# A two-block network on one core: how small work is spread between the weight products

## The chip, the cores and the metric

One Trainium2 chip, one core. The time is the device time of one execution, in microseconds (us). Before the change: median 1421.77 us of 3 runs (1421.32 to 1427.34). TensorE is PE, its weight loads PEld, VectorE DVE, ScalarE ACT, GpSimd POOL, SyncE SP.

## The reference

Two transformer blocks run one after the other on 256 tokens of width 1024; each has 2 layers, all in float32.

```
first block, per layer:
  z = rmsnorm(h) @ w_in + b_in          # conv, pool, q, k, v, gates, index
  ya = conv31 -> layer norm -> silu -> matmul, times silu(gate)
  yb = windowed mean - value -> group matmul, times silu(gate)
  yc = attention over the 64 keys of highest index score, times silu(gate)
  h += concat(ya, yb, yc) @ w_out
  h += (p @ ple_w) * sigmoid(h @ ple_gate_w)
  at the end h = rmsnorm(h)
second block, per layer (x: 256 tokens, ctx: 256 tokens):
  mod = silu(c) @ w_ada + b_ada
  u = modulate(rmsnorm(x)) @ w_in
  gated linear attention (forward and backward), short conv, neighbourhood attention
  x += g1 * concat(...) @ w_out
  x += g2 * convffn(modulate(rmsnorm(x)))
  the same for ctx in layer 0; at the end x = rmsnorm(x)
```

## The kernel before

Features lie on the partitions, tokens along the free axis (T = 256). Each float32 product is made of three products of rounded parts (`mm3`, L387 to L390: high by high, high by the rest of the data, rest of the weight by high). Weights arrive in units of 128x1024 float32 (512 KB) that SP loads into a ring of 4 (`rawunit`, L425); ACT copies a unit to its high part (L441) and DVE subtracts to get the rest (`hl`, L449). This subtraction is called the split. A tile of the output is 24 products (8 blocks of the inner size, three each). The third product of a block (L390) needs the split; the first two need ACT's copy alone.

Beside these tiles there is small work: in the first block the convolution (31 taps of two DVE operations each, `conv1`, L951), the pooling, the index scores and the attention; in the second the linear attention (`gla`, L1466) and the neighbourhood attention (`na`, L1666). Each is a generator that yields a number, its portion's cost. After every weight tile the main loop calls `tick` (L467), which runs portions until a budget is used:

```
    def tick(s, budget=1500.0, feed=True):
        ...
        while budget > 0 and s.tasks:
            for g in list(s.tasks):
                ...
                    c = next(g)
                ...
                if c is not None:
                    budget -= c
```

What is left is drained by `until` and by `flush` (L496), with no weight tile between its portions. So the budget, the yields and the place of a `tick` set how small work and weight tiles follow each other, and a tile framework then orders each engine's instructions; a "pinned" instruction keeps its place.

In the first block's `layer1` (L738) the last eight tiles of the input projection are gates (loop over j, a tick after each). Then w_out is applied in two halves of its inner size: g=0 takes the four blocks that are ready early, g=1, after `flush`, the convolution and the last attention heads. Each half adds its own result to h.

The sums of squares for the norms (`sumsq_add`, L528) are squares by ACT and additions `sqa` (L537), at the second block's residual by POOL; POOL takes the power -0.5 (L519). The merge of the linear attention (about L1650) adds both directions, squares, reduces over 64 columns (`gss`), takes the power on POOL (`grr`), multiplies (`slO`, L405) and transposes the tile on PE (L1660).

## Time and profile before

| | before |
|---|---|
| median of 3 runs | 1421.77 us |
| profiled execution | 1419.99 us |
| its span | 1418.2 us |
| granted clock, mean | 0.984 |
| PE busy | 1363.1 us (96%), 10658 products |
| DVE busy | 1126.9 us (79%) |
| ACT busy | 675.8 us (48%) |
| POOL busy | 69.1 us (5%) |

The profile comes from one execution. Busy time is the time with an instruction in work; a wait is idle time on an engine with the instruction that ended it. PE is the engine with the least idle time, so the list of its waits is the list of what can be had without taking products away. The granted clock is 1.00 where PE runs at 2.4 GHz and 0.50 where it runs at 1.2 GHz.

### The profile page before, as it was taken

Reading aid. Unit: us, or ns where it says so; the run is one execution under the profiler, and the core shown is the slowest. Engines: PE = TensorE matmul, PEld = TensorE weight load, DVE = VectorE, ACT = ScalarE, POOL = GpSimd, SP = SyncE. Lnnn points to the kernel's source line nnn. Section 1 sums busy time; section 2 is a strip of 40 time slices with the busy share of each in tenths; the row PEclk is TensorE's granted clock in tenths of the full one; section 3 lists DMA queues with packets and bytes.
Section 4 is the critical chain, followed back from the end, with each engine's and each line's share of the span. In section 5 each row is a group of like instructions: output and inputs, shape, how many; then the busy total and the mean of one; then the engine's idle time right before and its main releaser. Section 6 shows DMA issues by size and latency. Waiting matters only on the chain.

```text
span 1418.2 us, 26810 instructions
## 1 busy us (share of the span) xinstructions
PE 1363.1 (96%) x10658; PEld 1167.0 (82%) x10658; DVE 1126.9 (79%) x2382; ACT 675.8 (48%) x1258; POOL 69.1 (5%) x98
## 2 busy tenths in 40 slices
PE   8999899997999998999999999999999999999997
PEld 7878799787988776778888888888788877999997
DVE  6998669997889776888788977888767556798794
ACT  4446465464763343546444313343255446565562
POOL 0000000000100001011000000001210000100001
PEclk9999899998999999999999999999999999999999
DMA  7974256333643433432444564557732232376562
GB/s 263 333 248 132 90 164 219 108 118 120 208 148 121 137 100 97 143 102 80 143 137 153 159 189 149 165 183 254 231 117 91 92 116 89 119 217 195 183 194 73
DMA packets 63909, 219.02 MB, mean 154 GB/s; under 512 B 7270, under 2 KB 12328, under 8 KB 63528
## 3 DMA queue, kind: packets, MB, share of 16 engines
q1 hardware_dynamic: 58368, 209.22, 45.9%
q10 hardware_dynamic: 5416, 8.09, 1.7%
q8 instruction: 84, 1.38, 0.4%
q14 instruction: 41, 0.34, 0.1%
HBM read 216.23 MB, written 1.05 MB: 153 GB/s over the span
## 4 chain that ended last, share of the span: by engine, by line
PE 71%; DVE 14%; issue 6%; DMA 4%; ACT 3%; POOL 2%; ACTq 0%; POOLq 0%; DVEq 0%
PE mm L388 20%; PE mm L389 19%; PE mm L390 19%; PE ax L385 8%; DVE hl L449 3%; DMA wada<-in_wadaT_dram 2%; PE mm L385 1%; DVE wada L683 1%; DMA raw<-in_units_dram 1%; PE ada L385 1%; DVE gU L396 1%; PE ax L1744 1%; ACT hl L441 1%; DVE x L396 1%; POOL sqa L537 1%
## 5 line engine op out<-in xcount | busy, mean ns | idle before, releaser
L388 PE MATMUL mm<-xx,hl 128*128 128x256 f32 (+1 forms) x1720 | 555.5, 325 | 5.5 <-ACT xx L414 2.0
L390 PE MATMUL mm<-xx,hl 128*128 128x256 f32 (+1 forms) x1720 | 545.5, 318 | 1.5 <-DVE hl L449 1.4
L389 PE MATMUL mm<-xx,hl 128*128 128x256 f32 (+1 forms) x1720 | 546.3, 318 | 0.0
L441 ACT ACTIVATE hl<-raw 128x1024 fp32r<-128x1024 f32 x286 | 301.4, 1055 | 189.1 <-PE mm L390 152.0
L449 DVE TENSOR_TENSOR hl<-raw,hl 128x1024 fp32r<-128x1024 f32 x286 | 349.4, 1223 | 46.8 <-ACT hl L441 45.2
L388 PEld LDWEIGHTS mm<-xx,hl 128*128 128x128 f32 x1720 | 324.7, 189 | 50.2 <-issue 16.7
L390 PEld LDWEIGHTS mm<-xx,hl 128*128 128x128 f32 x1720 | 325.4, 190 | 30.3 <-DVE hl L449 3.1
L389 PEld LDWEIGHTS mm<-xx,hl 128*128 128x128 f32 x1720 | 325.7, 190 | 27.7 <-issue 4.7
L396 DVE SCALAR_TENSOR_TENSOR y<-mm,sp,y 128x255 f32<-128x255 f32 (+1 forms) x184 | 109.1, 595 | 31.4 <-ACT y L409 30.1
L389 PE MATMUL mm<-hid,hl 128*128 128x256 f32 (+1 forms) x374 | 124.8, 334 | 0.0
L388 PE MATMUL mm<-hid,hl 128*128 128x256 f32 (+1 forms) x374 | 124.0, 332 | 0.0
L390 PE MATMUL mm<-hid,hl 128*128 128x256 f32 (+1 forms) x374 | 123.9, 331 | 0.0
L683 DVE CUSTOM_DVE_ANT_0 wada<-wada,crow,sp 128x1024 f32<-128x1024 f32 x80 | 103.9, 1305 | 10.7 <-DMA wada<-in_wadaT_dram 10.3
L409 ACT ACTIVATE y<-mm,sp 128x256 f32<-128x256 f32 (+1 forms) x92 | 60.6, 659 | 98.4 <-PE mm L390 98.3
L388 PEld LDWEIGHTS mm<-hid,hl 128*128 128x128 f32 x374 | 71.8, 192 | 7.7
L389 PEld LDWEIGHTS mm<-hid,hl 128*128 128x128 f32 x374 | 71.8, 192 | 6.7
L390 PEld LDWEIGHTS mm<-hid,hl 128*128 128x128 f32 x374 | 71.5, 191 | 6.9
L396 DVE SCALAR_TENSOR_TENSOR x<-mm,mod,x 128x256 f32<-128x256 f32 x96 | 43.7, 479 | 31.4 <-PE mm L390 31.4
L389 PE MATMUL mm<-hl,xx 128*128 128x416 f32 (+3 forms) x192 | 66.0, 346 | 2.5 <-DVE hl L449 2.5
L537 POOL TENSOR_TENSOR sqa<-sqa,sq 128x256 f32<-128x256 f32 x36 | 35.2, 986 | 673.9 <-ACT sq L409 673.0
L388 PE MATMUL mm<-hl,xx 128*128 128x416 f32 (+3 forms) x192 | 65.9, 349 | 0.1
L390 PE MATMUL mm<-hl,xx 128*128 128x416 f32 (+3 forms) x192 | 65.6, 344 | 0.0
(281 smaller groups left out, 1659.9 us busy)
## 6 DMA issues: line engine op xcount, KB each, us to landing
raw<-in_units_dram SPq DMA_DIRECT2D x296, 512.0 KB, 4.0
wada<-in_wadaT_dram SPq DMA_DIRECT2D x80, 512.0 KB, 3.6
wada<-in_wada_dram SPq DMA_DIRECT2D x16, 512.0 KB, 5.8
nab<-in_nab_dram ACTq DMA_DIRECT2D x12, 192.0 KB, 3.4
crow<-in_crow_dram SPq DMA_DIRECT2D x2, 1024.0 KB, 6.7
x<-in_xT_dram SPq DMA_DIRECT2D x4, 256.0 KB, 5.2
x<-in_ctxT_dram ACTq DMA_DIRECT2D x1, 1024.0 KB, 10.7
c<-in_c_dram ACTq DMA_DIRECT2D x1, 928.0 KB, 5.5
```

What stands on the lines that cost most here:

```text
L385: return s.nc.tensor.matmul(out, lhsT, rhs, start=start, stop=stop, **kw)
L388: s.nc.tensor.matmul(out, l[0], r[0], start=start, stop=False)
L389: s.nc.tensor.matmul(out, l[0], r[1], start=False, stop=False)
L390: s.nc.tensor.matmul(out, l[1], r[0], start=False, stop=stop)
L396: s.nc.vector.scalar_tensor_tensor(out, a, sc, b, op0, op1)
L409: s.nc.scalar.activation(out, in_, func, bias=bias, scale=scale)
L441: a = nc.scalar.activation(hl[:, 0], raw, AF.Copy)
L449: b = nc.vector.tensor_sub(hl[:, 1], raw, hl[:, 0].bitcast(F32))
L537: (eng or s.nc.vector).tensor_tensor(st["acc"], st["acc"], sq, ALU.add)
L683: s.pin(nc.vector.tensor_tensor_reduce(out=w, in0=w, in1=c[:, j], scale=1.0, scalar=bias[:, m : m + 1], op0=ALU.mult, op1=ALU.add, accum_o ...
L1744: nc.tensor.transpose(pt[:, kt * 128 : kt * 128 + 128], L[j][:, kt * 128 : kt * 128 + 128], s.ident)
```

## The change

It has nine parts.

1. Gates of the first block: a tick has a budget of 2800 instead of 1500; the convolution yields after every second tap (1300) and no longer after each (900).
2. First block's w_out: `part` sums both halves in four PSUM banks (three named mm, one ada) that stay open from g=0 to g=1; h gets one addition of 128x512 per pair of output tiles, four in a layer and not sixteen of 128x256. Ticks stand in the first half alone.
3. The norm at the head of a layer works on pairs of blocks, 128x512.
4. The first loads: pinned; the first unit in two pieces; the second and fourth load of x through ACT's queue.
5. The context's sum of squares moves from the gates of layer 1 to the end of layer 0.
6. The last two additions of `sqa` at a residual's sum are made by DVE.
7. The merge of the linear attention yields 800, 700, 400 and 500 where it yielded 1500 and 700.
8. Neighbourhood attention yields 400 between the copies of the probabilities and the products with v, and 500 after them instead of 900.
9. At the end the scale is multiplied in by ACT during the last down projection, so the final step is four multiplications of 128x512. PAIR_PACE, the share of modulation work fed in beside the FFN's upper tiles, goes from 2.2 to 2.7.

```diff
-PAIR_PACE = 2.2
+PAIR_PACE = 2.7
-CONVY = 900
+CONVY = 1300
+GATE_TICK = 2800
-GZ = 1500
+GZ = 800
...
-    def rawunit(s):
+    def rawunit(s, pieces=1):
         u = s.u
         s.u += 1
         raw = s.wp.tile([128, 1024], F32, name=s.nm("raw"), tag="raw", bufs=NRAW)
-        s.nc.sync.dma_start(raw, s.dram[u])
+        n = 1024 // pieces
+        for o in range(0, 1024, n):
+            d = s.nc.sync.dma_start(raw[:, o : o + n], s.dram[u, :, o : o + n])
+            if pieces > 1:
+                s.pin(d)
         return raw
...
+    def part(s, out, hl, ks, off, g):
+        for q, k in enumerate(ks):
+            s_, e_ = not g and not off and q == 0, bool(g) and bool(off) and q == len(ks) - 1
+            r = [s.mv(e, k, 0, T) for e in range(2)]
+            kw = dict(skip_group_check=True)
+            s.mm(out, hl[:, 0, o : o + 128], r[0], s_, False, **kw)
+            s.mm(out, hl[:, 0, o : o + 128], r[1], False, False, **kw)
+            s.mm(out, hl[:, 1, o : o + 128], r[0], False, e_, **kw)
...
-        s.raw0 = []
-        for k in range(0, KT, 2):
-            nc.sync.dma_start(s.h[:, k : k + 2], xT[:, k : k + 2])
-            if k in RAW0:
-                s.raw0.append(s.rawunit())
+
         s.sp1 = s.small1(0)
+        load = lambda q, k: s.pin(q.dma_start(s.h[:, k : k + 2], xT[:, k : k + 2]))
+        load(nc.sync, 0)
+        s.raw0 = [s.rawunit(2)]
+        load(nc.scalar, 2)
+        load(nc.sync, 4)
+        load(nc.scalar, 6)
+        s.raw0.append(s.rawunit())
...
-            for k in range(KT):
-                n = s.t([128, T], "nf", 2, pool=s.sm)
-                s.tt(n, gh[:, k], rs, ALU.mult)
-                s.split(s.xx[:, 1, 0, k], s.xx[:, 1, 1, k], n)
+            for k in range(0, KT, 2):
+                n = s.t([128, 2, T], "nh", 2)
+                s.tt(n, gh[:, k : k + 2], rs.unsqueeze(1).to_broadcast([128, 2, T]), ALU.mult)
+                s.split(s.xx[:, 1, 0, k : k + 2], s.xx[:, 1, 1, k : k + 2], n)
...
         if i == DEPTH - 1:
-            sc = {}
-            for k in range(KT):
-                s.sumsq_add(sc, s.x2[:, k, :T], 2, k == 0, k == KT - 1)
-            rc = s.rstd_cols(sc["ps"][:, 0:2], 2, 1.0 / D, "rc")
...
-            s.tick()
+            s.tick(GATE_TICK)
...
+        wo = [s.bank("mm" if b < 3 else "ada") for b in range(4)]
         for g in range(2):
             if g:
                 s.turns = False
                 s.flush()
-            for m in range(KT):
-                if m % 2 == 0:
-                    hl = s.unit()
-                ps = s.mtile(0, T, hl, WO_ORDER[4 * g : 4 * g + 4], m % 2 * 4)
-                s.tt(h[:, m], h[:, m], ps[:, :T], ALU.add)
+            for m in range(0, KT, 2):
+                hl, ps = s.unit(), wo[m // 2]
+                for d in range(2):
+                    s.part(ps[:, d * T : d * T + T], hl, WO_ORDER[4 * g : 4 * g + 4], d * 4, g)
+                    if not g:
+                        s.tick()
                 if g:
-                    s.split(s.xx[:, 1, 0, m], s.xx[:, 1, 1, m], h[:, m])
-                s.tick()
+                    hm = h[:, m : m + 2]
+                    s.tt(hm, hm, ps.rearrange("p (k t) -> p k t", k=2), ALU.add)
+                    s.split(s.xx[:, 1, 0, m : m + 2], s.xx[:, 1, 1, m : m + 2], hm)
...
+            if i == DEPTH - 2:
+
+                s.sumsq_add(sc, s.x2[:, m, :T], 2, m == 0, m == KT - 1)
+                if m == KT - 1:
+                    s.rc = s.rstd_cols(sc["ps"][:, 0:2], 2, 1.0 / D, "rc")
...
-            yield CONVY
+            if k % 2 == 0:
+                yield CONVY
...
-            for k in range(KT):
-                y = s.x2[:, k, T:]
-                s.stt(y, y, s.sp2[0]["fin"][:, k : k + 1], R[:, :T], ALU.mult, ALU.mult)
-                if k % 2:
-                    q = nc.sync if k % 4 == 1 else nc.scalar
+            for k in range(0, KT, 2):
+                y = s.x2[:, k : k + 2, 0:T]
+                s.tt(y, y, R[:, :T].unsqueeze(1).to_broadcast([128, 2, T]), ALU.mult)
+                q = nc.sync if k % 4 else nc.scalar
...
-                s.sumsq_add(st[j], s.x2[:, m, c], 2, m == 0, m == KT - 1, eng=s.nc.gpsimd if SQP[1] else None)
+                s.sumsq_add(st[j], s.x2[:, m, c], 2, m == 0, m == KT - 1,
+                            eng=s.nc.gpsimd if SQP[1] and m < KT - 2 else None)
...
+                if half and not both:
+
+                    s.a(s.x2[:, m, 0:T], s.x2[:, m, T:], AF.Copy, scale=P["fin"][:, m : m + 1])
...
             yield 700
             rr = s.rstd_cols(ss, 6, 1.0 / 64, "gr")
+            yield 400
             s.tt(o3, o3, rr.unsqueeze(2).to_broadcast([128, 6, 64]), ALU.mult)
+            yield 500
...
                 s.a(PT[j][:, :kw], pt[:, :kw], AF.Copy)
+            yield 400
 
             for kt in range(nkt):
                 for j in range(2):
...
-            yield 900
+            yield 500
```

Three places show how the order of instructions moves. The first is DVE in the gates of layer 0: the rows that end with the split of the fifth gate (`hl_1196` before, `hl_1231` after). `acc` are the taps, `aL` the attention's scores, `py` the pooling, `sil` the gates. Before:

```order
153 L449 TENSOR_TENSOR hl_1123<-raw_1121,hl_1123 128x1024
154 L396 SCALAR_TENSOR_TENSOR sil_942<-th_974,zh_973 128x256
155 L1077 ISA aL_987,amx_986<-ax_984,imk_696 128x128
156 L1077 ISA amx_986 128x1
157 L1077 ISA aL_987,amx_986<-ax_985,imk_696 128x128
158 L1077 ISA amx_986 128x1
159 L396 SCALAR_TENSOR_TENSOR acc_390<-u_206,sp_80,acc_390 128x256 x2
160 L1091 RECIPROCAL asm_1051<-asm_1051 128x2
161 L449 TENSOR_TENSOR hl_1196<-raw_1194,hl_1196 128x1024
```

After:

```order
178 L1104 ISA aL_1153,amx_1152<-ax_1151,imk_689 128x128
179 L1104 ISA amx_1152 128x1
180 L406 TENSOR_TENSOR py_1139<-py_1139,sil_943 128x256
181 L397 SCALAR_TENSOR_TENSOR acc_375<-u_191,sp_72,acc_375 128x256 x3
182 L416 TENSOR_TENSOR xx<-py_1139,xx 128x256
183 L397 SCALAR_TENSOR_TENSOR acc_375<-u_191,sp_72,acc_375 128x256 x3
184 L406 TENSOR_TENSOR yc_1221<-ax_1080,sil_943 128x256
185 L397 SCALAR_TENSOR_TENSOR sil_943<-th_1196,zh_1195 128x256
186 L397 SCALAR_TENSOR_TENSOR acc_375<-u_191,sp_72,acc_375 128x256 x2
187 L454 TENSOR_TENSOR hl_1231<-raw_1229,hl_1231 128x1024
```

Ahead of this split DVE has 62 taps after the change and 30 before, the remaining heads' first scores, and the pooling's products; in layer 1 likewise 32 more.

The second place is PE at w_out in layer 0. `csq`, `clr`: the layer norm of the convolution; `sw`: its projection; `aL`, `aPT`, `v`: the attention; `hl_1713`, `hl_1541`: units of w_out. Before, from the end of the first half to the start of the second:

```order
715 L390 MATMUL mm_1753<-xx,hl_1750 128x256
716 L385 MATMUL ax_1662<-c_82,csq_1660 128x1 x4
717 L385 MATMUL ax_1671<-c_82,clr_1669 128x128 x2
718 L385 MATMUL ax_1684<-csq_1660,sw_102 128x256
719 L385 MATMUL ax_1690<-csq_1660,sw_102 128x256
720 L1104 MATMUL ax_1696<-c_82,aL_1593 128x128
721 L385 MATMUL ax_1684<-csq_1660,sw_102 128x256
722 L385 MATMUL ax_1690<-csq_1660,sw_102 128x256
723 L1104 MATMUL ax_1696<-c_82,aL_1593 128x128 x3
724 L385 MATMUL ax_1624<-aPT_1701,v_816 64x128 x4
725 L388 MATMUL mm_1716<-xx,hl_1713 128x256
```

After, the same work and the first half:

```order
608 L386 MATMUL ax_1494<-csq_1295,sw_103 128x256 x2
609 L1131 MATMUL ax_1500<-c_83,aL_1432 128x128 x4
610 L386 MATMUL ax_1511<-csq_1295,sw_103 128x256 x2
611 L386 MATMUL ax_1527<-kr_606,qr_430 128x256
612 L386 MATMUL mm_1535<-xx,hl_1541 128x256
613 L386 MATMUL ax_1442<-aPT_1505,v_809 64x128 x4
614 L386 MATMUL ax_1528<-kr_606,qr_430 128x256
615 L386 MATMUL mm_1535<-xx,hl_1541 128x256 x11
616 L1131 MATMUL ax_1556<-c_83,aL_1454 128x128 x2
617 L386 MATMUL mm_1535<-xx,hl_1541 128x256 x4
618 L386 MATMUL ax_1561<-aPT_1559,v_809 64x128 x2
```

The norm's column sums (128x1) now stand within the sixth gate, the projection ahead of w_out, and the last heads between the products of w_out's first half; the second half follows the first directly.

The third place is DVE at the third merge of the linear attention in layer 0 of the second block, from the reduction `gss` to the multiplication by `grr`; `ada` and `wada` are modulation work. Before:

```order
976 L1654 TENSOR_REDUCE gss_6403<-slO_6401 128x6
977 L678 ISA ada_6641,mod_452<-wada_6639,crow_4500,mod_452 128x512
978 L678 ISA mod_452 128x1
979 L515 TENSOR_SCALAR grm_6405<-gss_6403 128x6
980 L683 ISA wada_6639,mod_452<-wada_6639,crow_4500,sp_249 128x1024
981 L683 ISA mod_452 128x1
982 L405 TENSOR_TENSOR slO_6297<-slO_6297,grr_6407 128x384
```

After:

```order
914 L1684 TENSOR_REDUCE gss_6308<-slO_6306 128x6
915 L698 ISA ada_6546,mod_445<-wada_6544,crow_4405,mod_445 128x512
916 L698 ISA mod_445 128x1
917 L520 TENSOR_SCALAR grm_6310<-gss_6308 128x6
918 L703 ISA wada_6544,mod_445<-wada_6544,crow_4405,sp_234 128x1024
919 L703 ISA mod_445 128x1
920 L406 TENSOR_TENSOR slO_6202<-slO_6202,grr_6312 128x384
```

Here nothing has moved, and PE has 27 products of 128x512 between the last product of the recurrence and the transposes, before and after.

## Rows read from the trace of the kernel before

**Rows 1.** Windows of the whole span: busy us and (instructions) per engine, clock, DMA share, GB/s

```profile
60.00:106.00 46.00, 46.00 (x360) 34.68 (x356) 45.92 (x123) 22.87 (x46) 0.00 (x0) 1.00 0.78 267
...
143.00:159.00 16.00, 11.01 (x51) 9.18 (x52) 6.52 (x18) 4.30 (x10) 0.70 (x1) 0.68 0.11 33
...
320.00:340.00 20.00, 12.73 (x59) 10.22 (x59) 12.16 (x24) 4.96 (x11) 1.61 (x1) 0.74 0.34 106
...
664.00:1018.00 354.00, 352.78 (x1599) 287.97 (x1598) 292.66 (x467) 131.97 (x173) 11.96 (x11) 1.00 0.54 173
...
sum 1418.20, PE 1363.06 PEld 1167.02 DVE 1126.93 ACT 675.76 POOL 69.12; mean PE 80.18 PEld 68.65 DVE 66.29 ACT 39.75 POOL 4.07
```

**Rows 2.** Waits of PE over the span: us in total, times, longest us

```profile
PE ax L1660 <- DVE slO L405: 8.8, 5, 2.8
PE ax L385 <- POOL sqa L537: 5.6, 5, 1.7
```

**Rows 3.** Waits of PE from 120 to 160 us, first and last

```profile
PE ax L385 <- DVE csq L396: 2.2, 1, 2.2
...
PE ax L385 <- ACT csq L409: 0.5, 1, 0.5
```

**Rows 4.** Waits of PE from 320 to 341 us, first and last

```profile
PE ax L385 <- DVE csq L396: 2.4, 1, 2.4
...
PE ax L385 <- DVE acc L396: 0.3, 1, 0.3
```

**Rows 5.** Windows inside the two bare stretches, columns as in rows 1

```profile
145.30:152.20 6.90, 4.73 (x13) 3.57 (x14) 2.23 (x7) 2.08 (x5) 0.00 (x0) 0.51 0.15 61
155.60:159.00 3.40, 3.40 (x17) 3.40 (x17) 0.85 (x2) 0.42 (x1) 0.00 (x0) 0.50 0.00 0
326.20:333.10 6.90, 4.51 (x12) 3.57 (x13) 3.81 (x8) 2.07 (x4) 0.00 (x0) 0.51 0.60 203
```

**Rows 6.** DVE by form from 60 to 140 us: count, busy us, mean ns

```profile
L396 DVE SCALAR_TENSOR_TENSOR acc<-u,sp,acc 128x256 f32<-128x256 f32 x39 | 17.2, 477 | 0.0
...
L405 DVE TENSOR_TENSOR x<-x,mm 128x256 f32<-128x256 f32 x7 | 2.9, 420 | 0.3 <-PE mm L390 0.3
```

**Rows 7.** DVE timeline: the fifth gate's split, layer 0 (start us, us)

```profile
93.34 1.21 DVE L449 TENSOR_TENSOR hl<-raw,hl 128x1024 fp32r<-128x1024 f32 x1
```

**Rows 8.** PE timeline: the fifth gate's first low-part product, layer 0

```profile
106.39 0.28 PE L390 MATMUL mm<-xx,hl 128*128 128x256 f32 x1
```

**Rows 9.** PE timeline: start of the output projection's second half, layer 0

```profile
155.05 0.38 PE L388 MATMUL mm<-xx,hl 128*128 128x256 f32 x1 [0.98 <-ACT xx L414]
```

**Rows 10.** DVE timeline: the fifth gate's split, layer 1

```profile
280.85 1.22 DVE L449 TENSOR_TENSOR hl<-raw,hl 128x1024 fp32r<-128x1024 f32 x1
```

**Rows 11.** PE timeline: the fifth gate's first low-part product, layer 1

```profile
284.69 0.38 PE L390 MATMUL mm<-xx,hl 128*128 128x256 f32 x1
```

**Rows 12.** PE timeline: start of the output projection's second half, layer 1

```profile
336.11 0.39 PE L388 MATMUL mm<-xx,hl 128*128 128x256 f32 x1 [0.98 <-ACT xx L414]
```

**Rows 13.** Timeline of the third merge's stretch: POOL's power and PE's transposes

```profile
546.50 2.33 POOL L519 TENSOR_TENSOR grr<-grm,mhalf 128x6 f32<-128x6 f32 x1 [22.35 <-DVE grm L515]
...
549.57 0.30 PE L1660 MATMUL ax<-c,slO 128*128 128x128 f32 x1 [2.76 <-DVE slO L405]
```

**Rows 14.** POOL by form from 600 us on: the sums of squares

```profile
L537 POOL TENSOR_TENSOR sqa<-sqa,sq 128x256 f32<-128x256 f32 x36 | 35.2, 986 | 673.9 <-ACT sq L409 673.0
```

**Rows 15.** PE timeline: the longest wait in the neighbourhood attention

```profile
1140.65 0.32 PE L385 MATMUL ax<-slO,bigC 128*64 128x128 f32 x1 [1.03 <-ACT slO L409]
```

**Rows 16.** Waits of SP's queue in the first 24 us

```profile
SPq L590 <- DMA sp<-in_sp_dram: 2.4, 1, 2.4
```

**Rows 17.** Timeline of the first 10 us: SP's issues

```profile
1.73 0.43 SPq L590 DMA_DIRECT2D x<-in_xT_dram  x1
```

**Rows 18.** PE timeline: the first weight product

```profile
7.17 0.45 PE L385 MATMUL mm<-sil,raw 128*128 128x256 f32 x1 [1.20 <-DMA raw<-in_units_dram]
```

**Rows 19.** Timeline of the end: the final multiplications

```profile
1411.52 3.22 DVE L396 SCALAR_TENSOR_TENSOR x<-x,sp,ax 128x256 f32<-128x256 f32 x8 [1.59 <-PE ax L385]
```

More of the change, by code (lines that the diff above doesn't have):

```diff
@@ L563, in mtile @@
         return ps
+    def part(s, out, hl, ks, off, g):
+        for q, k in enumerate(ks):
+            o = (q + off) * 128
+            s_, e_ = not g and not off and q == 0, bool(g) and bool(off) and q == len(ks) - 1
[4 more added lines that the diff above has]
+            s.mm(out, hl[:, 1, o : o + 128], r[0], False, e_, **kw)
     def ftile(s, x, keep=False):
@@ L587, in setup @@
         xT = A["xT"].rearrange("p (k t) -> p k t", k=KT)
-        s.raw0 = []
-        for k in range(0, KT, 2):
-            nc.sync.dma_start(s.h[:, k : k + 2], xT[:, k : k + 2])
-            if k in RAW0:
-                s.raw0.append(s.rawunit())
-        s.sp1 = s.small1(0)
+        s.sp1 = s.small1(0)
+        load = lambda q, k: s.pin(q.dma_start(s.h[:, k : k + 2], xT[:, k : k + 2]))
[5 more added lines that the diff above has]
+        s.raw0.append(s.rawunit())
         c0 = s.const.tile([128, 256], F32, name="c0", tag="c0")
-        nc.scalar.dma_start(c0, A["c0"])
+        s.pin(nc.scalar.dma_start(c0, A["c0"]))
         s.ident, s.ones = c0[:, 0:128], c0[:, 128:256]
         cc = s.const.tile([128, KT, 2], F32, name="cc", tag="cc")
-        nc.scalar.dma_start(cc, A["cc"].rearrange("p (k j) -> p k j", k=KT))
+        s.pin(nc.scalar.dma_start(cc, A["cc"].rearrange("p (k j) -> p k j", k=KT)))
         s.mhalf = s.const.tile([128, 32], F32, name="mhalf", tag="mhalf")
@@ L734, in small1 @@
         sp = s.t([128, s.A["sp1"].shape[2]], "sp1", 2)
-        s.nc.scalar.dma_start(sp, s.A["sp1"][i])
+        s.pin(s.nc.scalar.dma_start(sp, s.A["sp1"][i]))
         return {n: sp[:, o : o + w] for n, (o, w) in SP1.items()}
@@ L888, in layer1 @@
             if i == DEPTH - 1 and j == RCTX:
-                ps = s.spread(rc, 2)
+                ps = s.spread(s.rc, 2)
                 s.a(s.rctx, ps[:, :T], AF.Copy)
-            s.tick()
+            s.tick(GATE_TICK)
         s.pace = PACE[3]
@@ L921, in layer1 @@
         lastl = i == DEPTH - 1
+        sc = {}
         s.gh = None if lastl else s.t([128, KT, T], "sil", 1)
@@ L1153, in block2 @@
             R = s.spread(s.rstd_cols(s.st["ps"][:, 0:2], 2, 1.0 / D), 2)
-            for k in range(KT):
-                y = s.x2[:, k, T:]
-                s.stt(y, y, s.sp2[0]["fin"][:, k : k + 1], R[:, :T], ALU.mult, ALU.mult)
-                if k % 2:
-                    q = nc.sync if k % 4 == 1 else nc.scalar
-                    q.dma_start(s.out[:, k - 1 : k + 1], s.x2[:, k - 1 : k + 1, T:])
+            for k in range(0, KT, 2):
+                y = s.x2[:, k : k + 2, 0:T]
+                s.tt(y, y, R[:, :T].unsqueeze(1).to_broadcast([128, 2, T]), ALU.mult)
+                q = nc.sync if k % 4 else nc.scalar
+                q.dma_start(s.out[:, k : k + 2], y)
     def cols(s, j):
```

## The prediction

> **What bounds the kernel now.** I read the windows of the span first, then the list of PE's waits, then the waits inside the stretches where PE has little to do, and last the timelines around them. The windows [rows 1] show PE busy for 1363.06 of 1418.20 us, so at most 55 us can be had without removing products, and a part of that is not waiting but short gaps. In the FFN stretch (664 to 1018 us) PE has no gap to speak of, 352.78 of 354. In the gates of the first block (60 to 106) both PE (46.00) and DVE (45.92 of 46.00) are full: work that is added to DVE there delays something. Two short stretches are bare: 143 to 159 us with PE at 11.01 of 16 and clock 0.68, and 320 to 340 us with 12.73 of 20 and 0.74. These are the flush before the second half of w_out, in layers 0 and 1. The five waits there in layer 0 sum to 5.7 us, the first and last being 2.2 and 0.5 [rows 3], the seven in layer 1 to 7.3, from 2.4 to 0.3 [rows 4]. Behind them the clock is at its lower level, 0.51 (1.2 GHz), for 6.90 us with 4.73 us of products (so 2.4 us lost), again for 3.40 us (1.7 lost), and in layer 1 for 6.90 us with 4.51 us of products (2.2 lost) [rows 5]. Outside block one the largest entries are the merge of the linear attention, 8.8 us in five waits, and the sums of squares, 5.6 in five [rows 2].
>
> **Part 1 and 2: gates, convolution, w_out in layer 0.** The order shows what moves: 32 more taps, and some dozen smaller operations, stand ahead of the fifth gate's split on DVE, and on PE the layer norm of the convolution, its projection and the last heads stand between weight products. So the waits of 5.7 us lose their bareness and the clock its reason to fall. The price is DVE's. One tap is 17.2/39 = 0.44 us [rows 6], 32 are 14.1; the dozen others at up to 0.42 each (the addition in rows 6), less what the paired norm saves, I put at 3.0. The split began at 93.34 and ended at 94.55 [rows 7]; it now ends at 94.55 + 17.1 = 111.7. PE's first use of it was at 106.39 [rows 8], and 20 small products have moved ahead of that use: at 46.00/360 = 0.13 us a product [rows 1], 2.5 us, so PE is there at 108.9 and waits 2.8 us. From that use to the second half of w_out took 155.05 - 106.39 = 48.7 us [rows 8, 9]; less the waits 5.7, the lost clock 2.4 and the 2.5 that moved ahead leaves 38.0. So the second half starts at 149.7, 5.3 us earlier. The second fall of the clock (1.7) goes too, since no bare stretch is ahead of it, but the late splits bring short waits and perhaps a fall of the clock of their own; I set +1.5 against it: **-5.5**. Ends: all waits and both falls go and DVE hides the taps, -9.8; or splits of the later gates are late as well and nothing is left, +3.
>
> **The same in layer 1.** Here the split ended at 280.85 + 1.22 = 282.07 and was used at 284.69 [rows 10, 11]: 2.6 us of room where layer 0 had 11.8. DVE gets the taps' 14.1 us more ahead of it and 1.1 for the rest, since four or so additions of the context's sum of squares, at 0.42, have left this stretch; so the split ends at 282.07 + 15.2 = 297.3, while PE would be there at 284.69 + 2.5 = 287.2: PE stands for 10.1 us in the gates. From the use to the second half was 336.11 - 284.69 = 51.4 [rows 11, 12]; less 7.3 of waits, 2.2 of clock and 2.5 moved leaves 39.4, and the second half starts at 336.7, 0.6 late. The second fall goes (-1.7, priced as in layer 0), against +0.6 for falls at the gates: **-0.5**. Ends -11.2 (7.3 + 2.2 + 1.7) and +6 (two falls more and the ACT copies late). The four additions of 128x512 for sixteen of 128x256 are on DVE behind these splits and beside products; I count nothing for them.
>
> **The first loads.** SP's third load of x stands 2.4 us behind another transfer's landing [rows 16], and PE's first weight product waits 1.20 us for its weight [rows 18]. The first unit now comes in two pieces, and two loads of x leave SP's queue. Worth: nothing, if the first products then wait for something else; up to 3, if all early waits of PE go with the 2.4. I take one such wait: **-1.2**. The trace has one issue of a load at 0.43 us [rows 17], so two moved issues are 0.9 us of SP's time. The Trainium skill (DMA: Bandwidth & Descriptors, "Issuing engines are not separate DMA queues") says that starting transfers on several engines saves only the sequencer's issue time. By that rule this term would be at most 0.9 and the gain in all 0.3 us less; the 2.4 us that SP was held are a wait and not issue time, so this trace does not decide it.
>
> **Sums of squares.** POOL takes 986 ns for an addition [rows 14], DVE 420 [rows 6]. Two additions of each sum move, the last is on the path that PE waits for (5.6 us in five waits [rows 2]). If it is 0.45 us sooner in four places: **-1.8**; at most 2 x 0.57 in five places, -5.6, capped by the waits themselves; at worst 0, where DVE is busy when the square is ready.
>
> **Merge of the linear attention.** A new portion would have to bring PE work between POOL's power and the transposes. The third merge shows the wait: the power begins at 546.50 and takes 2.33 us, and PE's transposes at 549.57 have waited 2.76 [rows 13]. The order shows the same operations between reduction and multiplication on DVE and the same 27 products on PE. Only ahead of the first merge have two products of 512 columns come in: **-0.5**. Ends 0 and -8.8.
>
> **Neighbourhood attention.** Portions are cut finer; the waits are small, the longest 1.03 us [rows 15], and copies of the probabilities now have work behind them: **-1.0**, between +1 (the last portions come later) and -2.
>
> **The end.** Eight multiplications take 3.22 us [rows 19]; four of twice the width with one operand less I put at 2.5 to 2.6: **-0.6**, with ends 0 and -1.2. PAIR_PACE costs nothing while PE is full in the FFN and DVE is at 292.66 of 354 us [rows 1]; if a split comes late there, it is up to +2.
>
> **Sum.** -5.5 - 0.5 - 1.2 - 1.8 - 0.5 - 1.0 - 0.6 = -11.1. The profiled execution took 1419.99 us (span 1418.20), so 1408.9. It stands 1.8 us below the median of the runs, 1421.77; I set that difference back: **1410.7 us**.
>
> **Rivals.**
> *Gates bound by DVE in both layers.* What flush loses, the gates take. For it: DVE is full from 60 to 106 [rows 1]. Against: in layer 0 the split has 11.8 us of room [rows 7, 8]. Then layer 0 gives 0 and layer 1 +2; the rest, -5.1, stays: -3.1, 1418.7 us, no change that can be measured.
> *Slower: PE stops at each late gate and runs at its lower clock after it.* Place: gates three to seven of both layers. For it: the clock is at 0.51 behind waits of about 2 us [rows 3 to 5]. Price: 5 us of standing more per layer than I count, and two falls at 2.4 each, 9.8 per layer, 19.6 - 11.1 = +8.5: 1430.3 us. Forecast has 2.8 + 10.1 = 12.9 us of standing for splits; the gain is gone when these are 24.0, and it is slower measurably beyond 31. Against: after the fifth gate DVE has less than before to do, so later splits catch up.
> *Better: the taps do not delay the splits by as much as I count, and bare stretches go whole.* Layer 0 -9.8, layer 1 -11.2, the rest -5.1: -26.1, 1395.7 us. For it: sums of DVE time assume DVE full throughout; against, the windows show that it is [rows 1].
> *The merge's waits go.* 8.8 instead of 0.5: 1402.4 us. Against it stands the unchanged order there: the change doesn't do there what its words say.
>
> **How the numbers follow.** About 0.5% (7.1 us) is what a measurement of this kernel can tell from no change; faster means under 1414.7, slower over 1428.9. Forecast 0.55 (its own range 1404 to 1417), DVE-bound 0.18, slower 0.09, better 0.13, merge 0.05. Faster: 0.50 of the forecast's 0.55, and the last two, 0.18, so 0.68 and a little of the DVE-bound case, 0.69; same 0.21; slower 0.10. The range reaches from between the better case and the merge's to above the DVE-bound one: 1398 to 1421.
>
> **What would show it.** In the profile after: no clock below 0.9 in the stretch before w_out's second half in layer 0, no waits for csq and clr there, and PE waits for the split in layer 1's gates of about 10 us and in layer 0's of about 3. If the gates show no waits for splits, the DVE sum was too high, and the time is nearer 1396; if csq and clr are still waited for, the gain of layer 0 fails. Waits for slO stay near 8.3 us. If the multiplication by grr no longer holds PE, that step is wrong. A sum of squares still waited for over 1.5 us would show that the last additions were not what held it.

## The result, and the profile after

The changed kernel takes 1408.89 us (median of 4 runs, 1404.32 to 1410.06) against 1422.62 for the kernel before (4 runs, 1421.32 to 1427.34). The ratio is 0.9884, 95% interval 0.9851 to 0.9918: 1.2% faster, with 1410.7 predicted. Its profiled execution has a span of 1408.3 us, 9.9 less than before. The two profiled executions lie apart from the medians (2.6 us below for the kernel before, 1.2 above for the changed one), so the stretches below account for 9.9 of the 13.7 us between the medians.

The total came out nearly as predicted, yet several terms did not. The waits of PE over the span of the changed kernel (in total, times, longest):

```profile
PE ax L1692 <- DVE slO L406: 8.8, 5, 2.8
PE mm L390 <- DVE hl L454: 7.7, 5, 2.9
PE ax L386 <- POOL rsr L524: 3.3, 4, 1.6
PE mm L389 <- ACT hl L446: 2.6, 2, 2.0
PE ax L386 <- DVE sqa L542: 2.4, 3, 1.2
PE mm L389 <- ACT wada L410: 2.1, 1, 2.1
```

Against [rows 2], slO is unchanged to the tenth, sqa has fallen from 5.6 to 2.4 (0.9 of it a wait at the very first norm that the kernel before doesn't have), and hl by DVE, the wait for a weight's split, is now the second entry.

A total hides where time moves, so I align both traces at points of the program: the start of the first low-part product (the third product of a block, rest of the weight by high) that uses the n-th split. Between the same two points both programs have the same weight products to do; small work can have moved from one stretch to another. The column "again" is a second profile of the changed kernel, the same program run once more (see the experiments): what it differs by is scatter between executions.

| stretch | before | after | change | predicted | again |
|---|---|---|---|---|---|
| start to 9th split | 53.32 | 58.17 | +4.85 | -1.2 | 57.25 |
| to 34th: rest of layer 0 with gates and w_out | 113.72 | 107.57 | -6.15 | -5.5 | 107.47 |
| to 44th: end of layer 0, norm of layer 1 | 42.79 | 44.50 | +1.71 | 0 | 44.40 |
| to 87th: layer 1 | 167.21 | 161.33 | -5.88 | -0.5 | 161.67 |
| to 131st: second block's first mixers, FFN's start | 333.92 | 333.40 | -0.52 | -1.9 | 334.90 |
| to 185th: first FFN | 300.15 | 300.15 | 0.00 | 0 | 300.15 |
| to 189th: end of that FFN, next norm | 28.27 | 21.28 | -6.99 | -0.4 | 21.28 |
| to 221st: second mixers | 185.30 | 183.53 | -1.77 | -1.0 | 184.94 |
| to 286th: last FFN | 180.53 | 185.13 | +4.60 | 0 | 180.67 |
| to the end | 12.99 | 13.22 | +0.23 | -0.6 | 13.05 |

(The predicted terms for sums, merges and attention are spread over their places.) The changes sum to -9.9, the difference of the spans. The +1.71 has its other side in layer 1: part 5 moves eight column sums of the context on PE from there to the end of layer 0, where PE is busy 1.3 us longer. The prediction put nothing in for it.

Three places of the changed trace. First the start: windows (columns as in rows 1) around the 30th us, and ACT's timeline (start, length, operation, in brackets what it waited for).

```profile
28.00:32.00 4.00, 0.51 (x2) 0.30 (x2) 3.72 (x10) 4.00 (x6) 0.00 (x0) 0.94 0.61 190
32.00:36.00 4.00, 3.73 (x17) 3.74 (x18) 4.00 (x5) 0.54 (x1) 0.00 (x0) 0.50 0.85 263
```

```profile
23.89 0.49 ACT L410 ACTIVATE th<-yc,halfb 128x256 f32<-128x256 f32 x1
27.77 0.47 ACT L410 ACTIVATE ki<-mm,sp 128x256 f32<-128x256 f32 x1 [3.38 <-PE mm L391]
...
28.64 2.95 ACT L446 ACTIVATE hl<-raw 128x1024 fp32r<-128x1024 f32 x3
```

ACT stands 3.38 us for ki, the eviction (copy out of PSUM) of a tile that PE is still computing, and behind it in ACT's order stand the copies of the next weight units. PE then has 0.51 us of work in four, and 1.2 GHz (0.50) in the four behind.

Second, the fifth gate's split and the products that bound it: DVE and PE in layer 0, then in layer 1, then the start of w_out's second half in each.

```profile
118.49 1.22 DVE L454 TENSOR_TENSOR hl<-raw,hl 128x1024 fp32r<-128x1024 f32 x1
```

```profile
119.76 0.39 PE L391 MATMUL mm<-xx,hl 128*128 128x256 f32 x1 [0.40 <-DVE hl L454]
...
154.63 0.39 PE L386 MATMUL mm<-xx,hl 128*128 128x256 f32 x2
...
297.33 0.38 PE L391 MATMUL mm<-xx,hl 128*128 128x256 f32 x1 [0.40 <-DVE hl L454]
...
331.70 0.28 PE L386 MATMUL mm<-xx,hl 128*128 128x256 f32 x1
```

```profile
296.06 1.22 DVE L454 TENSOR_TENSOR hl<-raw,hl 128x1024 fp32r<-128x1024 f32 x1
```

DVE was not full ahead of the split in layer 0. These are two of four waits there, 4.3 us in all (the others 0.84 for PE and 0.81 for ACT):

```profile
98.94 0.55 DVE L403 TENSOR_SCALAR py<-ax,sp 64x256 f32<-64x256 f32 x1 [1.44 <-PE ax L386]
...
108.17 1.12 DVE L403 TENSOR_SCALAR py<-ax,sp 64x256 f32<-64x256 f32 x2 [1.20 <-PE ax L386]
```

Beside [rows 7 to 12]: the split is ready 25 and 15 us later than before, PE's use of it is 13 and 13 us later, and still the second half starts earlier by 0.4 and 4.4, since nothing bare is left between. (The kernel before has run nine products of the second half ahead of its bare stretch, which the rows at 155.05 and 336.11 don't show. At the first low-part product that both still have to run, 155.89 and 336.97 before, the changed kernel is 0.02 and 4.02 us earlier.) In the windows over w_out in the changed kernel PE is full and the clock whole, where [rows 1] had 11.01 of 16 and 12.73 of 20:

```profile
139.80:165.70 25.90, 25.80 (x223) 24.38 (x223) 17.11 (x29) 12.05 (x19) 0.00 (x0) 1.00 0.49 155
318.40:342.80 24.40, 24.36 (x214) 23.60 (x213) 16.79 (x27) 12.32 (x20) 0.00 (x0) 1.00 0.49 152
```

Third, the end of the first FFN, from the 185th split's use to the 189th's, before and after:

```profile
1011.10:1039.40 28.30, 24.64 (x162) 23.68 (x161) 20.02 (x40) 7.96 (x15) 5.88 (x17) 0.88 0.47 148
```

```profile
1005.10:1026.40 21.30, 20.84 (x160) 20.61 (x159) 13.66 (x30) 7.33 (x14) 3.14 (x15) 1.00 0.28 92
```

DVE has 6.4 us less to do there, and PE's waits and its falls to the lower clock (0.88 in the mean before, 1.00 after) have gone.

### The profile page after: what moved, and what is told of

Same layout as the page of the kernel before. It is cut to its first block, busy times and chain, and to the rows that moved or that the text cites. A ratio compares the mean times of both kernels' runs of the same rounds, so it can differ in the third digit from the quotient of the medians.

```text
span 1408.3 us, 26751 instructions
## 1 busy us (share of the span) xinstructions
PE 1361.9 (97%) x10658; PEld 1168.0 (83%) x10658; DVE 1117.8 (79%) x2336; ACT 674.5 (48%) x1250; POOL 63.5 (5%) x92
## 3 DMA queue, kind: packets, MB, share of 16 engines
HBM read 216.23 MB, written 1.05 MB: 154 GB/s over the span
## 4 chain that ended last, share of the span: by engine, by line
PE 78%; DVE 12%; issue 4%; ACT 3%; POOL 2%; DMA 1%; ACTq 0%; POOLq 0%; DVEq 0%
PE mm L389 21%; PE mm L391 21%; PE mm L390 21%; PE ax L386 8%; PE mm L386 4%; DVE hl L454 3%; PE ada L386 1%; DVE acc L397 1%; DVE gU L397 1%; POOL sqa L542 1%; ACT hl L446 1%; ACT slA L412 1%; DVE wada L703 1%; PE ax L1776 1%; DVE ada L698 1%
## 5 line engine op out<-in xcount | busy, mean ns | idle before, releaser
L389 PE MATMUL mm<-xx,hl 128*128 128x256 f32 (+1 forms) x1592 | 521.1, 328 | 3.1 <-ACT wada L410 2.1
L391 PE MATMUL mm<-xx,hl 128*128 128x256 f32 (+1 forms) x1592 | 513.4, 323 | 1.7 <-DVE hl L454 1.7
L390 PE MATMUL mm<-xx,hl 128*128 128x256 f32 (+1 forms) x1592 | 512.6, 323 | 0.3 <-DVE xx L416 0.2
L389 PEld LDWEIGHTS mm<-xx,hl 128*128 128x128 f32 x1592 | 303.5, 191 | 48.4 <-issue 19.9
L391 PEld LDWEIGHTS mm<-xx,hl 128*128 128x128 f32 x1592 | 301.9, 190 | 30.3 <-DVE hl L454 3.3
L390 PEld LDWEIGHTS mm<-xx,hl 128*128 128x128 f32 x1592 | 302.2, 190 | 26.9 <-issue 3.8
L389 PEld LDWEIGHTS mm<-hid,hl 128*128 128x128 f32 x374 | 70.3, 188 | 7.7
L391 PEld LDWEIGHTS mm<-hid,hl 128*128 128x128 f32 x374 | 70.5, 188 | 6.8
L390 PEld LDWEIGHTS mm<-hid,hl 128*128 128x128 f32 x374 | 70.5, 188 | 6.7
L390 PE MATMUL mm<-hl,xx 128*128 128x416 f32 (+3 forms) x192 | 68.3, 358 | 7.7 <-DVE hl L454 7.7
L389 PE MATMUL mm<-hl,xx 128*128 128x416 f32 (+3 forms) x192 | 67.6, 357 | 2.0 <-ACT hl L446 2.0
L391 PE MATMUL mm<-hl,xx 128*128 128x416 f32 (+3 forms) x192 | 67.7, 354 | 0.0
L542 POOL TENSOR_TENSOR sqa<-sqa,sq 128x256 f32<-128x256 f32 x30 | 31.4, 1054 | 658.5 <-ACT sq L410 657.7
```

Source lines behind the costliest of these rows:

```text
L389: s.nc.tensor.matmul(out, l[0], r[0], start=start, stop=False)
L390: s.nc.tensor.matmul(out, l[0], r[1], start=False, stop=False)
L391: s.nc.tensor.matmul(out, l[1], r[0], start=False, stop=stop)
L542: (eng or s.nc.vector).tensor_tensor(st["acc"], st["acc"], sq, ALU.add)
```

## The experiments

Each is an edit to the changed kernel if nothing else is said, and is read at the points of the table. Ratios are to the kernel before, with their 95% intervals. How much one stretch scatters shows in layer 1: eight profiles of the changed kernel and the experiments have the same order of PE's, DVE's and ACT's instructions there and take 161.3 to 163.9 us, most of the difference in the gates ahead of the fifth. A difference of that size in one profile is no evidence.

**The first 60 us: old loads.**

```diff
-        load(nc.sync, 0)
-        s.raw0 = [s.rawunit(2)]
-        load(nc.scalar, 2)
...
+        for k in range(0, KT, 2):
+            nc.sync.dma_start(s.h[:, k : k + 2], xT[:, k : k + 2])
+            if k in RAW0:
+                s.raw0.append(s.rawunit())
```

> The changed kernel with the first loads as before (part 4 undone: order, queues, pieces, pins). Theory: the changed kernel loses 4.8 us in its first 60 us because on ACT the eviction of ki now stands ahead of the copies of the second to fourth unit, and that order comes only where the new loads and the paired norm meet. With the old loads one copy stands ahead of ki again; the first use of the ninth split (58.2 us in the changed kernel, 53.3 before) comes at 53 to 55, no product at half clock between 28 and 40 us, and the time falls by 3 to 5 us against the changed kernel. Rival: the paired norm alone delays the splits; then the ninth split stays near 58.

Ratio 0.9865 (0.9827 to 0.9903). The ninth split is used at 55.83, where 53 to 55 was expected and the changed kernel has 58.17 and 57.25: about half of the loss goes. The median, 1406.76 us, doesn't tell it from the changed kernel. PE still does little from 32 to 36 us, but keeps its clock:

```profile
28.00:32.00 4.00, 3.09 (x24) 2.67 (x22) 4.00 (x9) 1.56 (x3) 0.00 (x0) 1.00 1.00 360
32.00:36.00 4.00, 1.31 (x10) 1.31 (x11) 3.09 (x4) 2.90 (x3) 0.00 (x0) 1.00 0.94 331
```

The half that stays is another wait. ACT's copies stand for units that have not landed, and PE for such a copy:

```profile
31.87 1.06 ACT L446 ACTIVATE hl<-raw 128x1024 fp32r<-128x1024 f32 x1 [2.00 <-DMA raw<-in_units_dram]
33.58 1.06 ACT L446 ACTIVATE hl<-raw 128x1024 fp32r<-128x1024 f32 x1 [0.65 <-DMA raw<-in_units_dram]
```

```profile
34.69 0.39 PE L389 MATMUL mm<-xx,hl 128*128 128x256 f32 x1 [3.09 <-ACT hl L446]
```

So the rival, the paired norm by itself, fits this half.

**The first 60 us: single norm.**

```diff
-            for k in range(0, KT, 2):
-                n = s.t([128, 2, T], "nh", 2)
...
+            for k in range(KT):
+                n = s.t([128, T], "nf", 2, pool=s.sm)
+                s.tt(n, gh[:, k], rs, ALU.mult)
...
```

> The changed kernel with the norm at the head of a layer by single blocks as before (part 3 undone), the new loads kept. Theory (order of ki and the copies): the order of before returns, the early loads keep their gain of about 1.3 us, so the first use of the ninth split comes at 52 to 53 and the time falls 5 to 6 us below the changed kernel, to about 1403. Rival: the loss comes from the loads on ACT's queue (the fourth load of x, waited for 1.6 us); then the ninth split stays near 58 and the time near 1409, or worse by the eight small DVE operations that come back.

Ratio 0.9857 (0.9822 to 0.9891). The ninth split is used at 53.88: 4.3 us of the 4.85 are back (3.4 against the second profile's 57.25), with the loads of the changed kernel kept, so the loads on ACT's queue are not by themselves the cause. ACT's order has a copy ahead of ki again, and PE goes on:

```profile
26.18 1.05 ACT L446 ACTIVATE hl<-raw 128x1024 fp32r<-128x1024 f32 x1
...
27.80 0.48 ACT L410 ACTIVATE ki<-mm,sp 128x256 f32<-128x256 f32 x1 [0.18 <-PE mm L391]
28.18 2.04 ACT L446 ACTIVATE hl<-raw 128x1024 fp32r<-128x1024 f32 x2
```

The expected gain of the early loads (52 to 53) is not there. Layer 1 takes 163.82 us, 2.5 more than in the changed kernel; 1.05 of it stands in the first two units, where the norm is (7.07 us, not 6.02), the rest is within the scatter. The kernel as a whole, 1406.72 us where about 1403 was expected, is not clearly better than the changed one.

**The end of the first FFN: PAIR_PACE.**

```diff
-PAIR_PACE = 2.7
+PAIR_PACE = 2.2
```

> The changed kernel with PAIR_PACE at 2.2 as before. Theory: the 7.2 us won around the end of the second block's first FFN come from the modulation work that is fed in earlier and no longer stands on DVE there; so from the last FFN unit (1011) to the next layer's first unit PE takes 7 us longer again (waits for sqa and rsr, two falls of the clock), and the 2.1 us wait for ACT at the start of that FFN goes; the time is 4 to 6 us longer than the changed kernel's. Rival: the gain comes from the last two additions of the sum on DVE (part 6); then this stretch stays as in the changed kernel and the time within 2 us.

1419.83 us, ratio 0.9947 (0.9925 to 0.9969); its runs lie from 1411 to 1424, so the time alone doesn't bear the size. The stretch does: it takes 29.00 us again, and DVE's work and the fallen clock are back. The wait of 2.1 us for ACT at the FFN's start did not go as expected; one of 2.48 for DVE stands in its place.

```profile
1003.50:1032.50 29.00, 23.80 (x166) 22.87 (x165) 20.76 (x43) 8.25 (x15) 4.98 (x15) 0.94 0.47 148
```

**The same stretch: sums on POOL.**

```diff
-                            eng=s.nc.gpsimd if SQP[1] and m < KT - 2 else None)
+                            eng=s.nc.gpsimd if SQP[1] else None)
```

> The changed kernel with all additions of the residual's sums on POOL as before (part 6 undone). Theory: PE waits for sqa 0.5 to 1.2 us longer in four places, total 2 to 4 us, of it under 1 at the end of the first FFN. Rival (part 6 made the 7.2 us at the end of that FFN): that stretch is 6 to 7 us longer and so is the time.

Ratio 0.9868 (0.9831 to 0.9905). The stretch takes 21.9 us, so the additions did not make the 7 us:

```profile
1004.30:1026.10 21.80, 21.02 (x159) 20.59 (x159) 12.92 (x28) 7.30 (x13) 4.96 (x17) 1.00 0.30 93
```

Waits for sqa are 4.0 us in all (3.1 for POOL, 0.9 for DVE) and not 2.4. But PE waits 0.6 us less for rsr, the power that follows the sum (2.7 us in three waits, not 3.3 in four). Part 6 is worth 1.0 us of waits by that; the time doesn't resolve it.

**The gates as before.**

```diff
-CONVY = 1300
-GATE_TICK = 2800
+CONVY = 900
+GATE_TICK = 1500
...
-            if k % 2 == 0:
-                yield CONVY
+            yield CONVY
```

> The changed kernel with part 1 undone: a gate's tick 1500 and a yield of 900 after each tap. Only 33 taps then stand ahead of the fifth gate's split and the layer norm of the convolution stands bare ahead of w_out's second half. Theory (the order of the convolution is what part 2 needs): the first use of the fifth gate's split comes 8 to 9 us earlier in layer 0 and 8 to 12 in layer 1, but from there to the next stage PE takes 12 to 15 us longer with waits for clr and csq and a clock of 0.5; each layer loses 4 to 7 us, the time 8 to 14 us. Rival (w_out's open banks alone bring it, the taps' place is worth nothing since DVE is full either way): time within 3 us of the changed kernel's.

Ratio 0.9922 (0.9895 to 0.9949), 1416.98 us. The fifth gate is reached 8.5 us sooner in layer 0, and from there to the 34th split takes 60.10 us and not 45.98; layer 0 is 5.6 us longer, layer 1 3.1. The bare stretches are there again:

```profile
145.00:165.00 20.00, 15.12 (x83) 13.00 (x82) 6.86 (x16) 5.50 (x10) 0.70 (x1) 0.74 0.17 53
325.00:345.00 20.00, 14.83 (x72) 12.40 (x71) 8.59 (x19) 5.50 (x10) 0.87 (x1) 0.66 0.27 100
```

So part 1 carries layer 0's gain (5.6 of 6.15), even with w_out's banks open, and about half of layer 1's (3.1 of 5.88). What makes the other half was not tried; 1.0 of it stands at the paired norm (6.02 us for the first two units, 6.98 before), and the context's column sums have left the layer.

**w_out as before.**

```diff
-        wo = [s.bank("mm" if b < 3 else "ada") for b in range(4)]
...
+                ps = s.mtile(0, T, hl, WO_ORDER[4 * g : 4 * g + 4], m % 2 * 4)
+                s.tt(h[:, m], h[:, m], ps[:, :T], ALU.add)
```

> The changed kernel with part 2 undone: each half of w_out is added to h by itself, 16 additions of 128x256 a layer. The taps stay ahead of the fifth gate's split. Theory: the waits in flush stay away, since the convolution is done; DVE has some 4 us more work a layer beside w_out's products and a tick more in the second half; a layer loses 0 to 2 us. Rival (the open banks carry the gain): each layer loses 4 us or more from the fifth gate to the next stage.

Ratio 0.9849 (0.9822 to 0.9877), 1406.77 us. From the 9th to the 34th split it takes 107.49 us (107.57 with part 2), from there to the 87th 207.84 (205.83). The 2.0 us lie ahead of layer 1's fifth gate, where the order of PE's, DVE's and ACT's instructions is the same with and without part 2, so they are scatter. Part 2 by itself shows no worth in either layer, nor in the time. The rival falls.

**Paired norm in layer 1 alone.**

```diff
-            for k in range(0, KT, 2):
+            if i:
+                for k in range(0, KT, 2):
...
+            else:
+                for k in range(KT):
...
```

> The changed kernel with the paired norm in layer 1 alone, single blocks in layer 0. From the first two experiments: the first 60 us as with single blocks (first use of the ninth split near 53.9), 1.4 us lost again until the fifth gate, layer 1 as in the changed kernel: 3.5 to 4 us less than the changed kernel. Rival: the difference of the first stretch is eaten in the gates, where DVE is full: 0 to 1.5 us less.

1402.11 us, ratio 0.982 (0.9788 to 0.9851). The ninth split is used at 54.66 and the 87th at 367.57, 4.0 us before the changed kernel and 3.2 before its second profile: the head's loss is cut and not eaten in the gates.

**A smaller budget in the gates**, on top of the last one:

```diff
-GATE_TICK = 2800
+GATE_TICK = 2400
```

> As the kernel with the paired norm in layer 1 alone, with the gates' tick at 2400 instead of 2800: 8 taps fewer (3.5 us of DVE) ahead of the fifth gate's split in both layers, the column sums of the convolution's norm one gate later. Theory (in layer 1 PE stands for DVE in the gates): the fifth gate's first use comes 2 to 4 us earlier in layer 1 and the next stage 1 to 3 us earlier, in layer 0 no change. Rival: the taps that stand later make w_out's second half wait as much, no gain or a loss of 1 to 3 us.

1403.73 us, ratio 0.983 (0.9802 to 0.9858). The rival held: in layer 1 the fifth gate's use comes 2.9 us sooner than with 2800, of it all is lost and 2.1 more (within the scatter) by the 77th split's use (stretch from the 65th to the 77th 50.50 us, not 45.49). In the gates of layer 1 PE stands for DVE, but the taps that are put off must be paid ahead of w_out's second half.

**The changed kernel once more.**

> The changed kernel once more, nothing altered. In its first profile the products of 128x256 in the last FFN took 118 ns each instead of 113, 4.4 us in all; three of the other experiments that share this code had it, four did not or in half of it. Theory: it is a state of an execution and not of the code; the second profile may show 113 to 114 ns and a span near 1404. Rival: it belongs to this instruction order; then it is there again and the span is 1408 within 1 us.

1407.55 us, ratio 0.9869 (0.9835 to 0.9903). The same instructions: 223 products of 128x256 in 25 us of the last FFN, where the first profile of this code had 214 (the first fence is the first profile, the second the repeat):

```profile
1235.00:1260.00 25.00, 25.00 (x214) 25.00 (x213) 23.79 (x43) 16.69 (x28) 0.00 (x0) 1.00 0.68 207
```

```profile
1235.00:1260.00 25.00, 25.00 (x223) 25.00 (x222) 24.38 (x45) 16.89 (x28) 0.00 (x0) 1.00 0.72 215
```

The +4.60 of the last FFN in the table belongs to that execution and not to the change. The span is 1405.8 and not 1404, since the two stretches of mixers took 1.5 and 1.4 us longer this time. In this series the kernel before has a median of 1426.70 (17 runs, 1419.88 to 1436.29), so the whole change is worth 19.2 us here and 13.7 in the first series.

**Merge and neighbourhood attention as before.**

```diff
-GZ = 800
+GZ = 1500
...
-            yield 400
             s.tt(o3, o3, rr.unsqueeze(2).to_broadcast([128, 6, 64]), ALU.mult)
-            yield 500
...
-            yield 400
...
-            yield 500
+            yield 900
```

> The changed kernel with parts 7 and 8 undone (yields of the merge and of neighbourhood attention as before). Theory: the portions move next to nothing there; waits for slO stay at 8.8 us within 0.5, the stretch from the second block's mixers to its FFN within 1 us, the time within 2 us of the changed kernel's. Rival (the finer portions gave the 3 us between the 106th and the 119th split): that stretch is 2 to 4 us longer.

1411.96 us, ratio 0.9894 (0.9845 to 0.9942). The waits for slO are 8.8 in five again, as the theory said. But the stretches of the mixers are longer by 3.5 and 2.4 us than in the first profile of the changed kernel, and the rival had 2 to 4. From the 106th to the 124th split, and from the 207th to the 221st, in the changed kernel and in this one:

```profile
506.80:655.50 148.70, 140.25 (x1285) 108.62 (x1284) 119.95 (x298) 68.25 (x173) 16.08 (x15) 0.97 0.34 113
1139.30:1209.90 70.60, 65.94 (x485) 56.01 (x484) 44.24 (x98) 36.68 (x80) 7.12 (x7) 1.00 0.37 118
```

```profile
506.50:658.70 152.20, 141.90 (x1324) 108.72 (x1323) 120.35 (x298) 68.91 (x175) 15.92 (x15) 0.98 0.34 110
1142.30:1215.30 73.00, 68.32 (x485) 57.59 (x484) 44.85 (x100) 36.53 (x81) 7.13 (x7) 0.98 0.36 114
```

In the second stretch both have 485 products, and PE is "busy" 2.4 us longer for them: it doesn't wait long before any, but products that follow each other less closely are counted as busy. Not all of this is shown to be parts 7 and 8. In the first stretch this kernel has 40 more products (1324, not 1285): small ones of the linear attention that the changed kernel runs ahead of the 106th split, 0.6 us. From the 87th to the 124th split, with the same products, it takes 287.3 us where ten profiles that keep both parts take 281.8 to 286.1 (mean 284.3), and the two of the kernel before with PAIR_PACE 2.2 and 2.7 take 285.9 and 288.0. In the second stretch the ten take 70.5 to 72.6 (mean 71.3), and these three 72.3 to 73.4. So the two parts together bring some 4 us, 2.8 and 1.6 by the means, about what the medians differ by (3.1 and 4.4 us). Which of the two brings it was not tried.

**PAIR_PACE alone, in the kernel before.**

```diff
-PAIR_PACE = 2.2
+PAIR_PACE = 2.7
```

> The kernel before with PAIR_PACE 2.7 and nothing else. Theory: the stretch from the end of the second block's first FFN to the next layer's first units takes 5 to 7 us less, the start of that FFN up to 2 us more, nothing else moves: 4 to 6 us less than before. Rival (the gain needs the additions on DVE as well): 0 to 2 us less.

1419.81 us, ratio 0.9945 (0.9918 to 0.9971). The stretch at the end of the first FFN takes 21.9 us instead of 28.3, without any other part of the change:

```profile
1014.60:1036.50 21.90, 21.11 (x161) 20.66 (x160) 12.92 (x28) 7.32 (x14) 5.05 (x17) 1.00 0.31 95
```

The profile's span, 1419.2, is not below the 1418.2 of before, since this execution had the slower products of the last FFN (185.10 us, not 180.53) and 4.3 us more in layer 1 and the first mixers, where nothing was edited; the medians differ by 6.9 us (1426.70 before in this series).

**Longer portions in the merge**, on top of the paired norm in layer 1 alone:

```diff
-            yield 700
+            yield 1600
             rr = s.rstd_cols(ss, 6, 1.0 / 64, "gr")
-            yield 400
+            yield 1600
```

> As the kernel with the paired norm in layer 1 alone, with the merge's yields at 1600, 1600 and 500 instead of 700, 400 and 500. The order then has 54, 36, 15, 15, 54 and 30 weight products between recurrence and transposes of the six merges instead of 17, 42, 27, 15, 28 and 27. Theory (the wait is what the products in between don't cover, 0.23 us each): the waits of the first and fifth merge go (1.5 and 1.8 us) and half of the sixth, the third grows by up to 2.8 us: 0 to 2 us less than with the old yields. Rival: the portions are worth nothing, the chain of POOL and DVE starts later as well.

1403.12 us, ratio 0.9829 (0.9793 to 0.9865). The waits for slO go from 8.8 in five to this:

```profile
PE ax L1698 <- DVE slO L406: 6.4, 3, 3.4
```

The first and fifth merge wait no more, the third waits 3.38 where it was 2.76; the sixth, with 30 products and not 27, was to lose half of its wait and has it still, 1.85 (1.57 before). The theory of the cover holds for the large steps; the total (1403.12 against 1402.11) doesn't tell the two kernels apart. Both are faster than the changed kernel in the median, by 4 to 7 us.

## Why the prediction was right, and where it was not

*Gates and flush, layer 0: right in mechanism and size* (-5.5 predicted, -6.15 measured), the size by luck. None of the waits for csq and clr is left, and the clock is 1.00 ahead of w_out's second half, as forecast. Without the 4.85 us of the start, that half begins at 154.63 - 4.85 = 149.8; 149.7 was predicted. (The five waits of layer 0 are six in the list; their sum, 5.7, stands.) Two errors cancel in it. The split was ready 3.2 us later than worked out (119.71 - 4.85 = 114.9, not 111.7): the sum had DVE full, and it stood 4.3 us for PE and ACT. And from its use to the second half it took 34.9 us and not 38.0. The term that was mis-sized is the work that has left this stretch, 2.5 us for 20 small products. By the traces 28 small products have left it, which held 3.4 us there, and 14 weight products, worth 2.4. Four of the 14 now stand ahead of the use; nine belong to the second half, which the kernel before had begun ahead of its bare stretch, so 155.05 was not quite its start. That PE would stand 2.8 us for the split was wrong, it stands 0.4: the 28 products ahead of the use take 5.7 us, not 2.5.

*Layer 1: right mechanism, wrong size* (-0.5, measured -5.88). The split's end was predicted at 297.3 and is at 297.28, with luck: the layer starts 0.4 us later than before, and the additions of the context's sum that were to leave its gates never stood there (the trace of before has no sqa from 209.8 to 284.7 us; they ran at the end of layer 0 already). And the second half starts at 331.7, not at 336.7: 34.4 us from the use, where 39.4 was the sum. The step that failed is the same term. The 28 small products that left this stretch held 4.1 us there and not 2.5, which is 1.6 of the five. The other 3.4 lie in the weight products: 14 fewer again, about 1.8, and the rest follow each other 8 ns closer in the mean (0.128 us, not 0.136); which short delays have gone there is not settled. The gates do pay: PE waits for splits 7.0 us there (10.1 predicted), in seven times, the longest 2.9.

*First loads: wrong sign* (-1.2, measured +4.85). The first product did start at 5.90 and not at 7.17, which is more than the 0.9 us of issue time: SP no longer stands for another landing ahead of its x loads [rows 16]. By the Trainium skill's rule (DMA: Bandwidth & Descriptors, "Issuing engines are not separate DMA queues") 0.9 would have been all; the traces speak for the wait that went, though the unit in two pieces went in with it; with the old loads it is 7.17 again. By the ninth split nothing of it is left (53.88 with new loads and single norm, 53.32 before). What I did not price is what the new order puts behind what: I costed part 3 (the paired norm) as saving DVE time, and did not look at ACT's order, where ki had come ahead of the next unit's copy. The single norm takes 3.4 to 4.3 us of the loss away, and with it ki goes behind a copy again. That it is ki's place, and not the pairing itself, that costs this is argued: with the old loads a copy stands ahead of ki too and half of the loss stays, there as PE's wait for a copy whose unit landed late. What delayed that unit is open.

*PAIR_PACE: priced at nothing, worth -7.0.* I looked at the FFN itself, where it is hidden indeed (300.15 us before and after). The step failed at the place after it: modulation work not done by then is drained at the end of the FFN, on DVE, ahead of the residual that PE waits for. The experiments with PAIR_PACE alone (-6.4) and without it settle it.

*Sums of squares* (-1.8): right mechanism, 1.0 us of waits by the experiment. The 5.6 us in [rows 2] fell further because one wait of 1.6, at the end of the first FFN, went with PAIR_PACE: with that alone sqa is at 4.0 in the kernel before. *Merge:* waits unchanged as the order said; the 0.5 for the first merge did not come (1.45 after, 1.50 before). *Neighbourhood attention and merge together* were priced at -1.5 and bring some 4 us by the experiment, spread in short gaps that a list of waits doesn't show. At the start of the first FFN 1.5 us is lost; the cause of this was not tried. *The end:* the four multiplications take 2.48 us (2.5 to 2.6 predicted), but the span's end does not move with them: the four products ahead of them ran at a granted clock of 0.50 this time (1.23 us, 0.71 before), and the span ends 3.99 us behind them, not 3.46.

Of the rivals, the gates bound by DVE came true in part in layer 1 only, none in full. That the sum was right is luck, errors cancelled: measured less predicted, the stretches of the table add up to +14.6 us (the start 6.05, the last FFN 4.60, three others) and to -13.4 (the first FFN's end 6.59, layer 1 5.38, two others).

## What to carry to other kernels

Align two traces at the same instructions and take the differences by stretch before believing a total: here the sum came within 2 us while four stretches were each off by 4.6 to 6.6. Take a second profile of the same kernel before explaining a stretch: one moved by 4.5 us between two profiles of one program. When an edit lets a scheduler reorder, look in each engine's order for an instruction that waits for a late producer and has come ahead of work that feeds the bottleneck; here one eviction stood 3.38 us ahead of three copies, and the edit that put it behind a copy won 3.4 to 4.3. Background work that is hidden at its place still has an end: look where its rest is drained.

## What the runs showed of the hardware

In the last FFN the products of 128x256 follow each other every 113.3 to 113.4 ns in some executions and every 117.8 ns in others, with the granted clock at 1.00 in both. The same kernel shows both (the changed kernel and its repeat), and two experiments changed over within that FFN. It is worth 4.4 to 4.6 us over that FFN, as much as several terms of this change. What sets it is not shown.
